# Eight more convolution taps on TensorE, and another address distance for the lower weight parts of the MLP

## The chip, the cores and the metric

The kernel runs on one core of one Trainium2 chip. The metric is device time in microseconds (us) for one launch; lower is better. The core's engines have an instruction queue each and run beside one another: TensorE (PE in the profile; its weight loads are shown apart as PEld), VectorE (DVE), ScalarE (ACT), GpSimd (POOL) and SyncE (SP), which here only issues the loads of the weights.

## The reference

A trunk of two layers over 256 tokens of width 2048, all in float32. Layer 0 mixes the tokens with a convolution module, layer 1 with latent attention; a squared-ReLU MLP of width 8192 follows each.

```python
def conv_module(h, w_pw1, b_pw1, w_dw, b_dw, ln_g, ln_b, w_pw2, b_pw2):
    u = h @ w_pw1 + b_pw1
    a, gate = jnp.split(u, 2, axis=-1)
    u = a * jax.nn.sigmoid(gate)
    u = lax.conv_general_dilated(          # causal, one filter of 31 taps per channel
        u, w_dw[:, None, :].astype(u.dtype), window_strides=(1,),
        padding=[(CONV_WIDTH - 1, 0)],
        dimension_numbers=("NWC", "WIO", "NWC"),
        feature_group_count=D_MODEL) + b_dw
    u = jax.nn.silu(layer_norm(u, ln_g, ln_b))
    return u @ w_pw2 + b_pw2
...
def sq_relu_mlp(h, w1, w2):
    return jnp.square(jax.nn.relu(h @ w1)) @ w2
...
    for layer in range(DEPTH):
...
        x = x + conv_module(...)           # layer 0; mla(...) in layer 1
        h = rms_norm(x, norm_mlp_g[layer])
        x = x + sq_relu_mlp(h, mlp_w1[layer], mlp_w2[layer])
    return rms_norm(x, final_norm_g)
```

## The kernel before

**Products in parts.** TensorE multiplies a stationary tile (128 x 128, loaded as weights, PEld) with a moving tile. Each float32 operand is split into an upper part `hi` (a copy rounded to fp32r by ScalarE) and a lower part `lo` (the remainder, a subtraction on VectorE, in the convolution mostly on GpSimd). A product is three matmuls: hi x hi, hi x lo, lo x hi. The weights stream in as `raw` tiles, three in rotation, and the parts have six buffers each (`WB`).

**Order of the work.** The order on each queue is written out by hand (`tc.manual_schedule()`), and each engine runs its own queue in that order; semaphores hold an instruction until its operands are there. Nothing is rearranged later.

**Convolution stage** (layer 0, up to about 222 us of the profile). The 2048 channels are 16 tiles of 128, c = 0 to 15. For each tile `conv_mm` does the first pointwise product (16 k-tiles x 2 halves x 3 matmuls of 128 x 256, lines 862 to 864). `glu` gates it into `ub`, a tile of 30 zeros and 256 tokens. Then the 31 taps of the filter: each tap multiplies `ub`, shifted by w, with one value per channel and adds it to a running sum. Most taps are one VectorE instruction each (`dve_tap`, line 964). Some products are made on ScalarE (`product`) and summed on GpSimd (`side_sum`); `n_side` says how many. VectorE works at up to two tiles by turns and carries a number of taps over into the next tile's turn: `rest(c)`, for the last three tiles `LAST_REST`.

The last tile, c = 15, is treated otherwise: its first 22 taps (`LAST_PE`) are matmuls on TensorE, in which the stationary tile is a diagonal matrix with the tap's 128 values (`diag`, ScalarE, line 902) and the moving tile is the shifted `ub`. These 22 products (line 912, each recorded as two matmuls) add up in the PSUM bank `last_sum`; eleven stand right after `start_sum(15)`, eleven after the transposes of tile 13. VectorE does the other taps, and line 961 adds the two sums. The transposes to token order (`to_tokens`, line 1002) and the statistics of the layer norm (`ln_stats`, line 1012, into `stats`) follow for each tile; `cn` is the tile in which ScalarE gathers the transposed result (line 1014). `keep_warm` (line 237) is a run of transposes without use.

**MLP** (both layers). `up_unit` makes one 128-wide block of the first product: eight matmuls with the upper weight part (line 519, moving tile 128 x 512, both parts of the activations side by side), sixteen with the lower part (line 517, 128 x 256) and eight more of line 519. There are 64 such units in each layer. `down_units` does the second product (lines 198 to 200, moving tile 128 x 512). While a matmul runs, the weight load of the next one runs beside it.

**Addresses.** `hi_lo` makes the lower part's tile 64 elements (256 bytes) longer than needed (`LO_GAP`), so that the part can start at any place `at` in it. In the built program these places lie at, modulo 256 bytes: `hi` and the start of the `lo` tiles 64; the activations `xt` 0 in the convolution and 64 in the MLP. "Distance" here is the address of the moving tile less that of the stationary tile, modulo 256. It is 192 in the convolution's products (0 - 64), 0 for line 519 and in the second product of the MLP (64 - 64), and 192 for line 517, where `at` is 16 elements: 64 - (64 + 64).

Of the kernel before, what the change touches and what calls it, by code (L numbers as in the profile page):

```python
# [45 lines left out]
WB = 6  # L46
LOOK = WB // 2 - 1
LAST_PE = 22
SIDE = 2
LAST_SIDE = (3, 6, 4)  # L50
JOIN = 14
LEAD = 7
REST = (16, 18, 22)
LAST_REST = (20, 17, 0)
FILL_AT = (5, 15)
ORDERS = "STSTSTOSTSTSTSTT", "TSTSTSTOSTSTSTST"
N_S, N_G = 9, 2
# [28 lines left out]
def trunk_kernel(  # L86
# [336 lines left out]
    def hi_lo(n, at=0):  # L423
        hi = wpool.tile([P, n, NB], F32R, tag="hi", name=nm("hi"), bufs=WB)
        lo = wpool.tile([P, n * NB + LO_GAP], F32R, tag="lo", name=nm("lo"), bufs=WB)
        return [hi, lo[:, at : at + n * NB].rearrange("p (a b) -> p a b", b=NB)]
# [56 lines left out]
    def mlp(layer, ssq, next_gain, finish=None, before=None, last_w1=None):  # L483
# [11 lines left out]
        def up_units(hs, q, p, extra):  # L495
# [5 lines left out]
            def up_unit(b):  # L501
                ps = []

                def chunk(h):
                    def prep(raw, parts):
                        parts[h] = [a.rearrange("p a (j n) -> p (a j) n", n=P) for a in hi_lo(2, LO_GAP // 4)]
                        split_into(parts[h], raw[:, 8 * h : 8 * h + 8, :])

                    def run(parts):
                        if not ps:  # L510
                            ps.append(acc_tile())
                        wh, wl = parts.pop(h)
                        for low in (h, 1 - h):
                            for j in range(8):
                                k = 8 * h + j
                                if low:
                                    nc.tensor.matmul(ps[0][:, :S], wl[:, j, :], xh(k), start=False, stop=False)  # L517
                                else:
                                    nc.tensor.matmul(ps[0], wh[:, j, :], xhl(k), start=k == 0, stop=k == KC - 1)  # L519

                    def out():
                        if b == 0:
                            held["u"] = u_tile()
                        nc.scalar.activation(held["u"][:, b, :], ps[0], AF.Copy)  # L524

                    if h == 0:
                        return Chunk(prep, run)
                    return Chunk(prep, run, [add, lambda: None, square, forms, part] + extra if b == 1 else [], now=out)

                unit = Unit(rows(w1, 0, KC, ((q * NPAIR + p) * 2 + b) * P, P), KC, [chunk(h) for h in range(2)])  # L530
                unit.last_read = 1
                return unit
# [270 lines left out]
    with ExitStack() as cx:  # L803
# [94 lines left out]
            return pr  # L898

        def diag(c, w):  # L900
            dg = cv2.tile([P, P], F32, tag="dg", name=nm("dg"), bufs=LAST_PE)
            nc.scalar.activation(dg, ident, AF.Copy, scale=tap(c, w))
            return dg

        dgs, last_sum, turns = [], [], {}

        def last_products(w0, w1):  # L910
            for w in range(w0, w1):
                nc.tensor.matmul(  # L912
                    last_sum[0], dgs[w], ubs[KC - 1][:, w : w + S], start=w == 0, stop=w == LAST_PE - 1
                )

        def start_sum(c):
            w = 0
            if c < KC - 1:
                pcs[c] = sum_tile()[:, :S]
                nc.scalar.activation(  # L920
                    pcs[c], ubs[c][:, 0:S], AF.Identity, bias=b_dw[:, c : c + 1], scale=tap(c, 0)
                )
                w = 1
            else:
                pcs[c] = acc_tile()[:, :S]
                o = sum_tile()[:, :S]
                last_sum.append(o)
                last_products(0, LAST_PE // 2)
                w = LAST_PE
            n = n_side(c)  # L930
            sides[c] = [product(c, w + i) for i in range(n)]
            left[c] = list(range(w + n, W))
            left[c].insert(min(JOIN, len(left[c]) - 1), None)

        def side_sum(c):
# [7 lines left out]
        def dve_tap(c):  # L943
# [9 lines left out]
                )  # L953
                return
            if not left[c]:
                if c == KC - 1:
                    half = cv2.tile([P, S], F32, tag="half", name=nm("half"), bufs=1)
                    nc.vector.scalar_tensor_tensor(
                        out=half, in0=ubs[c][:, w : w + S], scalar=tap(c, w), in1=out, op0=ALU.mult, op1=ALU.add
                    )  # L960
                    nc.vector.tensor_tensor(ca_part(c), last_sum[0], half, op=ALU.add)
                    return
                out = ca_part(c)
            nc.vector.scalar_tensor_tensor(  # L964
# [64 lines left out]
        with tc.manual_schedule():  # L1029
# [57 lines left out]
            for c in range(1, KC + 1):  # L1087
                n = UC * c
                conv_load(n + 3)
                glu(c - 1)  # L1090
                fill = ln_stats(c - 4 if c < KC else KC - 3) if c > 3 else []
                fill, copies = fill[:T], fill[T:]
# [21 lines left out]
                if c < KC:  # L1114
                    conv_mm(c, 8)
                    if c > KC - 4:
                        dgs.extend(diag(KC - 1, w) for w in range(len(dgs), min(len(dgs) + 8, LAST_PE)))
                    if c > 2:
                        to_tokens(c - 3)
                    conv_mm(c, 12)  # L1120
# [673 lines left out]
```

## Time and profile before

| | us |
|---|---|
| median of 3 runs (lowest, highest) | 1934.97 (1933.55, 1935.04) |
| the profiled execution: its own time | 1933.95 |
| the profiled execution: span of the program | 1932.1 |
| TensorE busy in the span | 1903.0 (98%) |
| VectorE busy | 1650.8 (85%) |
| ScalarE busy | 1204.7 (62%) |
| GpSimd busy | 223.3 (12%) |

The profile is of one execution. "Busy" is the time in which an engine has an instruction under way; matmuls overlap, so a busy TensorE may still be issuing slower than it could, and the distance from one matmul's start to the next one's tells more than its duration. A row of the timeline gives start, duration, engine, line, operation, tiles (out<-in) and in brackets the idle time before and what ended it. "xN" merges N instructions that follow each other.

### The profile page before, as it was taken

The page shows a single profiled execution, that of the slowest core. Times are in us where ns is not written, and L with a number is a line of the kernel's source. Part 1 is how long each engine was busy: PE and PEld are TensorE (multiplying, and loading weights), DVE is VectorE, ACT ScalarE, POOL GpSimd, SP SyncE. Part 2 cuts the span into 40 slices and gives each one's busy share as a digit, 9 for nine tenths or more (in the row PEclk, how much of TensorE's full clock was granted, in tenths as well). Part 3 has the DMA queues.
Part 4 walks back from the last instruction along what each step waited for, and adds up shares of the span by engine and source line. Part 5 has one row for each costly group of instructions (what it writes and reads, how often), then busy time and mean ns, then how long its engine had stood idle before and what let it go on. Part 6 is the DMA issues. An engine that isn't in the chain of part 4 may idle for free.

```text
span 1932.1 us, 28479 instructions
## 1 busy us (share of the span) xinstructions
PE 1903.0 (98%) x10778; PEld 1669.4 (86%) x10778; DVE 1650.8 (85%) x2374; ACT 1204.7 (62%) x1709; POOL 223.3 (12%) x183
## 2 busy tenths in 40 slices
PE   7999899999999999999999999999999999999998
PEld 7999788888888888888899998888888888888886
DVE  5999865789999999999977665657999999999887
ACT  5556654766666666666566665566666666666554
POOL 5999300000000000000001410000000000000000
PEclk9999999999999999999999999999999999999999
DMA  8676355857666667666646445765666666766663
GB/s 235 187 195 179 129 189 160 227 170 213 197 203 206 201 198 215 198 199 214 199 144 182 121 153 175 203 188 173 199 195 209 207 196 196 217 199 196 213 220 109
DMA packets 407113, 367.62 MB, mean 190 GB/s; under 512 B 15416, under 2 KB 351936, under 8 KB 406720
## 3 DMA queue, kind: packets, MB, share of 16 engines
q1 hardware_dynamic: 405952, 363.63, 62.9%
q10 hardware_dynamic: 1024, 2.17, 0.3%
q8 instruction: 84, 1.38, 0.3%
q14 instruction: 53, 0.43, 0.1%
HBM read 363.68 MB, written 2.10 MB: 189 GB/s over the span
## 4 chain that ended last, share of the span: by engine, by line
PE 88%; DVE 9%; ACT 1%; POOL 1%; issue 0%; DMA 0%; SPq 0%; DVEq 0%; ACTq 0%; POOLq 0%
PE acc L519 24%; PE acc L198 15%; PE acc L199 15%; PE acc L200 15%; PE acc L517 13%; DVE sum L964 7%; PE acc L254 1%; PE sum L912 1%; DMA xs<-in_x 0%; ACT hi L172 0%; PE acc L863 0%; PE acc L862 0%; PE acc L864 0%; PE acc L1562 0%; PE acc L1426 0%
## 5 line engine op out<-in xcount | busy, mean ns | idle before, releaser
L430 DVE TENSOR_TENSOR lo<-raw,hi 128x1024 fp32r<-128x1024 f32 (+1 forms) x512 | 570.9, 1122 | 88.5 <-ACT hi L429 88.1
L429 ACT ACTIVATE hi<-raw 128x1024 fp32r<-128x1024 f32 (+1 forms) x512 | 479.6, 970 | 66.5 <-PE acc L199 66.2
L519 PE MATMUL acc<-xt,hi 128*128 128x512 f32 x2048 | 503.2, 391 | 0.0
L519 PEld LDWEIGHTS acc<-xt,hi 128*128 128x128 f32 x2048 | 376.0, 188 | 72.7 <-ACT hi L429 0.3
L198 PE MATMUL acc<-hi,sh 128*128 128x512 f32 x930 | 362.7, 390 | 0.0
L200 PE MATMUL acc<-lo,sh 128*128 128x512 f32 x930 | 361.9, 389 | 0.0
L199 PE MATMUL acc<-hi,sl 128*128 128x512 f32 x802 | 312.0, 389 | 0.0
L517 PEld LDWEIGHTS acc<-xt,lo 128*128 128x128 f32 x2048 | 259.3, 189 | 9.8
L517 PE MATMUL acc<-xt,lo 128*128 128x256 f32 x2048 | 262.4, 281 | 0.0
L172 ACT ACTIVATE hi<-raw 128x1024 fp32r<-128x1024 f32 (+2 forms) x184 | 179.9, 1006 | 46.7 <-PE acc L199 43.0
L200 PEld LDWEIGHTS acc<-lo,sh 128*128 128x128 f32 x930 | 174.6, 188 | 36.3
L198 PEld LDWEIGHTS acc<-hi,sh 128*128 128x128 f32 x930 | 174.6, 188 | 35.9
L173 DVE TENSOR_TENSOR lo<-raw,hi 128x1024 fp32r<-128x1024 f32 (+2 forms) x118 | 132.7, 1145 | 68.4 <-ACT hi L172 62.5
L429 ACT ACTIVATE hi<-V 128x1024 fp32r<-128x1024 f32 x94 | 99.6, 1059 | 130.4 <-DVE V L725 123.2
L199 PEld LDWEIGHTS acc<-hi,sl 128*128 128x128 f32 x802 | 150.6, 188 | 31.1
L964 DVE SCALAR_TENSOR_TENSOR sum<-ub,w_dw,sum 128x256 f32<-128x256 f32 x400 | 162.8, 480 | 6.5 <-ACT sum L920 5.4
L173 POOL TENSOR_TENSOR lo<-raw,hi 128x1024 fp32r<-128x1024 f32 x66 | 157.6, 2406 | 23.5 <-ACT hi L172 22.9
L429 ACT ACTIVATE hi<-T 128x1024 fp32r<-128x1024 f32 x94 | 99.3, 1056 | 91.7 <-DVE T L713 66.8
L524 ACT ACTIVATE U<-acc 128x512 f32<-128x512 f32 x128 | 75.7, 592 | 111.9 <-PE acc L519 111.8
L862 PE MATMUL acc<-xt,hi 128*128 128x256 f32 x512 | 143.6, 280 | 0.0
L863 PE MATMUL acc<-xt,hi 128*128 128x256 f32 x512 | 142.2, 278 | 1.0 <-DVE xt L211 1.0
L864 PE MATMUL acc<-xt,lo 128*128 128x256 f32 x512 | 142.2, 278 | 0.6 <-POOL lo L173 0.6
(270 smaller groups left out, 2797.1 us busy)
## 6 DMA issues: line engine op xcount, KB each, us to landing
raw<-in_mlp_w SPq DMA_DIRECT2D x256, 1024.0 KB, 6.2
raw<-in_conv_w_pw SPq DMA_DIRECT2D x64, 512.0 KB, 5.5
raw<-in_conv_w_pw SPq DMA_DIRECT2D x16, 1024.0 KB, 5.1
raw<-in_mla_w_o SPq DMA_DIRECT2D x16, 1024.0 KB, 5.4
raw<-in_mla_w_kv_up SPq DMA_DIRECT2D x8, 1024.0 KB, 5.4
raw<-in_mla_w_in SPq DMA_DIRECT2D x8, 576.0 KB, 3.8
raw<-in_mla_w_in SPq DMA_DIRECT2D x4, 1024.0 KB, 6.9
raw<-in_mla_w_q_up SPq DMA_DIRECT2D x16, 256.0 KB, 4.9
```

The source lines that it names most:

```text
L172: nc.scalar.activation(hi, raw[:, js, :], AF.Copy)
L173: eng.tensor_tensor(lo, raw[:, js, :], hi.bitcast(F32), op=ALU.subtract)
L198: nc.tensor.matmul(ps, sh, mh, start=start, stop=False)
L199: nc.tensor.matmul(ps, sl, mh, start=False, stop=False)
L200: nc.tensor.matmul(ps, sh, ml, start=False, stop=stop)
L429: nc.scalar.activation(parts[0], src, AF.Copy)
L430: nc.vector.tensor_tensor(parts[1], src, parts[0].bitcast(F32), op=ALU.subtract)
L517: nc.tensor.matmul(ps[0][:, :S], wl[:, j, :], xh(k), start=False, stop=False)
L519: nc.tensor.matmul(ps[0], wh[:, j, :], xhl(k), start=k == 0, stop=k == KC - 1)
L862: nc.tensor.matmul(o, wh[:, bs], xh(k), start=k == 0, stop=False)
L863: nc.tensor.matmul(o, wh[:, bs], xl(k), start=False, stop=False)
L964: nc.vector.scalar_tensor_tensor(out=out, in0=ubs[c][:, w : w + S], scalar=tap(c, w), in1=pcs[c], op0=ALU.mult, op1=ALU.add)
```

## The change

**Convolution.** The last eight taps (w = 23 to 30, `BUT_ONE_PE`) of tile c = 14 leave VectorE. ScalarE makes eight more diagonal tiles, in turn c = 15, behind the last of those for tile 15. They have no buffers of their own: they lie in the last four column blocks of `cn` (two rows of blocks, eight tiles), which ScalarE fills with results only afterwards. TensorE does the eight products (`but_one_products`) behind the last pointwise product and ahead of those of tile 15, into a PSUM bank of their own. VectorE's last tap of tile 14 goes into `half`, and one addition joins it with that bank, as for tile 15 before. `LAST_REST` for turn 14 goes from 17 to 9, so that VectorE does as many steps in that turn as before (28) and eight fewer in the last turn.

**MLP.** In `up_unit`, `at` goes from 16 to 56 elements, so that the lower part starts at 32 modulo 256 and the distance of line 517 becomes 64 - 32 = 32. No instruction is added, removed or moved; VectorE's write of the lower part and TensorE's load of it have other addresses.

The lines of the file move by 1 ahead of the new code (line 887 is now 888, 517 is 518), by 5 and 6 within it (902 is now 907, 912 is 918), by 14 to 18 behind it (961 is now 975, 1012 is 1026). The rows below are from the built programs, where a name's number tells one buffer from the next.

On TensorE, at the end of the last pointwise product, before:

```order
L864 MATMUL acc_2768<-xt_102,lo_2789 128x256
L862 MATMUL acc_2769<-xt_102,hi_2788 128x256
L863 MATMUL acc_2769<-xt_102,hi_2788 128x256
L864 MATMUL acc_2769<-xt_102,lo_2789 128x256
L912 MATMUL sum_2954<-ub_2944,dg_2532 128x256
L912 MATMUL sum_2954<-ub_2944,dg_2534 128x256
L912 MATMUL sum_2954<-ub_2944,dg_2536 128x256
```

and now, with `acc_2952` as the bank for tile 14 and the diagonals in `cn`:

```order
L865 MATMUL acc_2768<-xt_102,lo_2789 128x256
L863 MATMUL acc_2769<-xt_102,hi_2788 128x256
L864 MATMUL acc_2769<-xt_102,hi_2788 128x256
L865 MATMUL acc_2769<-xt_102,lo_2789 128x256
L926 MATMUL acc_2952<-ub_2761,cn 128x256 x8
L918 MATMUL sum_2971<-ub_2961,dg_2532 128x256
L918 MATMUL sum_2971<-ub_2961,dg_2534 128x256
L918 MATMUL sum_2971<-ub_2961,dg_2536 128x256
```

The eight products stand between the last pointwise matmul and the first product of tile 15.

On VectorE, the end of the last turn before (`sum_2774` is tile 14's running sum, `acc_2953` tile 15's, `tr_2915` the transposes of tiles 12 and 13):

```order
L964 SCALAR_TENSOR_TENSOR sum_2774<-ub_2761,w_dw,sum_2774 128x256
L947 TENSOR_TENSOR acc_2953<-acc_2953,tp_2966 128x256
L964 SCALAR_TENSOR_TENSOR sum_2774<-ub_2761,w_dw,sum_2774 128x256
L1012 BN_STATS stats<-tr_2915 128x6
L964 SCALAR_TENSOR_TENSOR sum_2774<-ub_2761,w_dw,sum_2774 128x256
L1012 BN_STATS stats<-tr_2915 128x6
L964 SCALAR_TENSOR_TENSOR sum_2774<-ub_2761,w_dw,sum_2774 128x256 x5
L964 SCALAR_TENSOR_TENSOR ca_3021<-ub_2761,w_dw,sum_2774 128x256
L958 SCALAR_TENSOR_TENSOR half_3023<-ub_2944,w_dw,acc_2953 128x256
L961 TENSOR_TENSOR ca_3021<-sum_2954,half_3023 128x256
L1012 BN_STATS stats<-acc_3040 128x6 x2
```

and now (tile 15's running sum is `acc_2970`, the transposes of tiles 12 and 13 are `tr_2923`):

```order
L978 SCALAR_TENSOR_TENSOR sum_2774<-ub_2761,w_dw,sum_2774 128x256
L978 SCALAR_TENSOR_TENSOR acc_2970<-ub_2961,w_dw,acc_2970 128x256
L972 SCALAR_TENSOR_TENSOR half_3027<-ub_2761,w_dw,sum_2774 128x256
L975 TENSOR_TENSOR ca_3029<-acc_2952,half_3027 128x256
L961 TENSOR_TENSOR acc_2970<-acc_2970,tp_2983 128x256
L1026 BN_STATS stats<-tr_2923 128x6
L972 SCALAR_TENSOR_TENSOR half_3033<-ub_2961,w_dw,acc_2970 128x256
L975 TENSOR_TENSOR ca_3029<-sum_2971,half_3033 128x256
L1026 BN_STATS stats<-tr_2923 128x6
L1026 BN_STATS stats<-acc_3051 128x6 x2
```

Eight taps of tile 14 are gone, one addition (`ca_3029<-acc_2952,half_3027`) is new, and one of the two statistics of `tr_2923` now stands behind the addition that waits for `last_sum`.

On ScalarE, at the gate of tile 15 (`sg`), before:

```order
L902 ACTIVATE dg_2909<-ident,w_dw 128x128
L902 ACTIVATE dg_2911<-ident,w_dw 128x128
L902 ACTIVATE dg_2913<-ident,w_dw 128x128
L884 ACTIVATE sg_2946<-acc_2769,vecs_cv 128x256
L172 ACTIVATE hi_2949<-raw_2633 128x1024
L897 ACTIVATE tp_2966<-ub_2944,w_dw 128x256
```

and now:

```order
L907 ACTIVATE dg_2909<-ident,w_dw 128x128
L907 ACTIVATE dg_2911<-ident,w_dw 128x128
L907 ACTIVATE dg_2913<-ident,w_dw 128x128
L907 ACTIVATE cn<-ident,w_dw 128x128 x8
L885 ACTIVATE sg_2963<-acc_2769,vecs_cv 128x256
L173 ACTIVATE hi_2966<-raw_2633 128x1024
L898 ACTIVATE tp_2983<-ub_2961,w_dw 128x256
```

The eight diagonals stand ahead of the gate's sigmoid. GpSimd's and SyncE's queues are as before.

```diff
--- before.py
+++ after.py
@@ -46,12 +46,13 @@
 WB = 6
 LOOK = WB // 2 - 1
 LAST_PE = 22
+BUT_ONE_PE = 8
 SIDE = 2
 LAST_SIDE = (3, 6, 4)
 JOIN = 14
 LEAD = 7
 REST = (16, 18, 22)
-LAST_REST = (20, 17, 0)
+LAST_REST = (20, 9, 0)
 FILL_AT = (5, 15)
 ORDERS = "STSTSTOSTSTSTSTT", "TSTSTSTOSTSTSTST"
 N_S, N_G = 9, 2
@@ -503,7 +504,7 @@
 
                 def chunk(h):
                     def prep(raw, parts):
-                        parts[h] = [a.rearrange("p a (j n) -> p (a j) n", n=P) for a in hi_lo(2, LO_GAP // 4)]
+                        parts[h] = [a.rearrange("p a (j n) -> p (a j) n", n=P) for a in hi_lo(2, LO_GAP - 8)]
                         split_into(parts[h], raw[:, 8 * h : 8 * h + 8, :])
 
                     def run(parts):
@@ -898,11 +899,16 @@
             return pr
 
         def diag(c, w):
-            dg = cv2.tile([P, P], F32, tag="dg", name=nm("dg"), bufs=LAST_PE)
+            if c == KC - 2:
+                t, j = divmod(w - W + BUT_ONE_PE, 4)
+                dg = cn[:, t, (KC - 4 + j) * P : (KC - 3 + j) * P]
+            else:
+                dg = cv2.tile([P, P], F32, tag="dg", name=nm("dg"), bufs=LAST_PE)
             nc.scalar.activation(dg, ident, AF.Copy, scale=tap(c, w))
             return dg
 
         dgs, last_sum, turns = [], [], {}
+        but_one, but_one_sum = [], []
 
 
 
@@ -911,6 +917,14 @@
             for w in range(w0, w1):
                 nc.tensor.matmul(
                     last_sum[0], dgs[w], ubs[KC - 1][:, w : w + S], start=w == 0, stop=w == LAST_PE - 1
+                )
+
+        def but_one_products():
+            but_one_sum.append(acc_tile()[:, :S])
+            for i, dg in enumerate(but_one):
+                w = W - BUT_ONE_PE + i
+                nc.tensor.matmul(
+                    but_one_sum[0], dg, ubs[KC - 2][:, w : w + S], start=i == 0, stop=i == BUT_ONE_PE - 1
                 )
 
         def start_sum(c):
@@ -929,7 +943,7 @@
                 w = LAST_PE
             n = n_side(c)
             sides[c] = [product(c, w + i) for i in range(n)]
-            left[c] = list(range(w + n, W))
+            left[c] = list(range(w + n, W - BUT_ONE_PE if c == KC - 2 else W))
             left[c].insert(min(JOIN, len(left[c]) - 1), None)
 
         def side_sum(c):
@@ -953,12 +967,12 @@
                 )
                 return
             if not left[c]:
-                if c == KC - 1:
+                if c >= KC - 2:
                     half = cv2.tile([P, S], F32, tag="half", name=nm("half"), bufs=1)
                     nc.vector.scalar_tensor_tensor(
                         out=half, in0=ubs[c][:, w : w + S], scalar=tap(c, w), in1=out, op0=ALU.mult, op1=ALU.add
                     )
-                    nc.vector.tensor_tensor(ca_part(c), last_sum[0], half, op=ALU.add)
+                    nc.vector.tensor_tensor(ca_part(c), (last_sum if c == KC - 1 else but_one_sum)[0], half, op=ALU.add)
                     return
                 out = ca_part(c)
             nc.vector.scalar_tensor_tensor(
@@ -1087,6 +1101,8 @@
             for c in range(1, KC + 1):
                 n = UC * c
                 conv_load(n + 3)
+                if c == KC:
+                    but_one_products()
                 glu(c - 1)
                 fill = ln_stats(c - 4 if c < KC else KC - 3) if c > 3 else []
                 fill, copies = fill[:T], fill[T:]
@@ -1115,6 +1131,8 @@
                     conv_mm(c, 8)
                     if c > KC - 4:
                         dgs.extend(diag(KC - 1, w) for w in range(len(dgs), min(len(dgs) + 8, LAST_PE)))
+                    if c == KC - 1:
+                        but_one.extend(diag(KC - 2, w) for w in range(W - BUT_ONE_PE, W))
                     if c > 2:
                         to_tokens(c - 3)
                     conv_mm(c, 12)
```

## The prediction

> **What bounds the kernel now.** I read the chain of waits and the groups first, then the windows, then the timeline at the two places that the change touches.
>
> ```profile
> PE 88%; DVE 9%; ACT 1%; POOL 1%; issue 0%; DMA 0%; SPq 0%; DVEq 0%; ACTq 0%; POOLq 0%
> L519 PE MATMUL acc<-xt,hi 128*128 128x512 f32 x2048 | 503.2, 391 | 0.0
> L517 PE MATMUL acc<-xt,lo 128*128 128x256 f32 x2048 | 262.4, 281 | 0.0
> 410.00:740.00 330.00, 330.00 (x1699) 283.12 (x1698) 316.65 (x374) 218.40 (x266) 0.00 (x0) 1.00 0.67 202
> ```
>
> The first row is the chain by engine, the next two are groups (count, busy time, mean duration, idle time before), the last is 330 us of the first MLP: its columns are PE, PEld, DVE, ACT and POOL busy, clock, DMA share, GB/s. TensorE carries the chain and never idles before the MLP's matmuls; its clock is full. So there a matmul's pitch, from one start to the next, sets the time. VectorE has 13.35 us left in 330 (4%). The chain of waits gives the pitch:
>
> ```profile
> 481.45 1.89 PE acc L517 x16
> 483.33 3.65 PE acc L519 x16
> 486.99 1.89 PE acc L517 x16
> ...
> 496.25 0.23 PE acc L198
> ...
> 499.88 0.23 PE acc L199
> ```
>
> Sixteen of line 517 take 483.33 - 481.45 = 1.88 to 1.89 us, so 117.8 ns each; sixteen of line 519 take 486.99 - 483.33 = 3.66, so 228.6 ns each; from 496.25 to 499.88 sixteen of the second product take 3.63, so 226.9 ns.
>
> A matmul of line 517's size does not always need 117.8 ns. In the convolution the timeline has:
>
> ```profile
> 159.73 0.28 PE L864 MATMUL acc<-xt,lo 128*128 128x256 f32 x1
> ...
> 163.81 0.28 PE L864 MATMUL acc<-xt,lo 128*128 128x256 f32 x1
> ...
> 175.62 0.28 PE L862 MATMUL acc<-xt,hi 128*128 128x256 f32 x1
> ...
> 182.45 0.28 PE L863 MATMUL acc<-xt,hi 128*128 128x256 f32 x1
> ```
>
> From 159.73 to 163.81 there are 36 starts, 113.3 ns each; from 175.62 to 182.45 there are 58, 117.8 ns each. Same line group, same shape, same distance (192), full clock: this matmul has a faster and a slower rhythm, and the stretch between two sets of transposes stays in one. Line 517, also at 192, stays in the slower.
>
> The convolution's end is the other place:
>
> ```profile
> 201.37 0.28 PE L864 MATMUL acc<-xt,lo 128*128 128x256 f32 x1
> 205.94 6.70 PE L912 MATMUL sum<-ub,dg 128*128 128x256 f32 x22 [4.29 <-DVE ub L887]
> 212.47 0.38 PE L1002 MATMUL tr<-ident,ca 128*128 128x128 f32 x2
> 212.69 4.92 PE L912 MATMUL sum<-ub,dg 128*128 128x256 f32 x22
> 217.45 1.03 PE L237 MATMUL acc<-ident 128*128 128x128 f32 x8
> ```
>
> TensorE idles 4.29 us until VectorE has made tile 15's `ub`. The first eleven products then take 212.47 - 205.94 = 6.53 us, the second eleven 217.45 - 212.69 = 4.76. The windows say why (PE busy, clock, DMA share, GB/s):
>
> ```profile
> 206.00:208.00 2.00, 2.00 (x7) 0.74 0.03 8
> 208.00:210.00 2.00, 2.00 (x6) 0.50 0.00 0
> 210.00:212.00 2.00, 2.00 (x10) 0.91 0.00 0
> ```
>
> The granted clock falls to half after the gap and comes back near 211.
>
> **Convolution part: cost.** TensorE: eight products at 4.76 / 11 = 0.433 us are 3.5 us, from 201.65 (201.37 + 0.28) to about 205.1, within the gap. Their cover is VectorE, which starts `ub` only then:
>
> ```profile
> 197.17 8.31 DVE L964 SCALAR_TENSOR_TENSOR sum<-ub,w_dw,sum 128x256 f32<-128x256 f32 x21
> 205.43 0.45 DVE L887 SCALAR_TENSOR_TENSOR ub<-acc,vecs_cv,sg 128x256 f32<-128x256 f32 x1
> 217.65 0.42 DVE L961 TENSOR_TENSOR ca<-sum,half 128x256 f32<-128x256 f32 x1 [0.20 <-PE sum L912]
> ```
>
> It steps through as many taps ahead of `ub` as before, so 205.43 stays. ScalarE's part:
>
> ```profile
> 184.61 2.44 ACT L902 ACTIVATE dg<-ident,w_dw 128x128 f32<-128x128 f32 x8
> 201.74 0.47 ACT L884 ACTIVATE sg<-acc,vecs_cv 128x256 f32<-128x256 f32 x1 [2.51 <-PE acc L864]
> 214.14 0.60 ACT L1014 ACTIVATE cn<-tr 128x512 f32<-128x512 f32 x1 [4.62 <-DVE stats L1012]
> 214.74 1.28 ACT L231 ACT_TABLE_LOAD   x1
> 219.81 0.60 ACT L1014 ACTIVATE cn<-acc 128x512 f32<-128x512 f32 x1 [3.57 <-DVE stats L1012]
> 220.46 0.20 ACT L221 ACTIVATE t<-v 128x2 f32<-128x2 f32 x1
> ```
>
> Eight diagonals cost 2.44 us in an idle stretch of 2.51 ahead of `sg`, which has 3.2 us to spare before `ub`. If that cover were gone, up to 2.44 us would fall on `sg`, still within its 3.2.
>
> VectorE drops seven instructions in the last turn (eight taps less, one addition more): 7 x 0.393 = 2.8 us, with (205.43 - 197.17) / 21 = 0.393 per tap. This gains nothing: line 961 already waits 0.20 us for TensorE, and does so longer now.
>
> What gains is the clock. With TensorE idle for under 1 us instead of 4.29 I expect no fall, so the first eleven products take 4.76 instead of 6.53: 1.77 us earlier at line 961. What is late next is ScalarE. It copies `cn` of tile 13 only after both its statistics (214.14 waits for VectorE), and one of them now stands behind line 961: 217.65 - 1.77 = 215.88, two instructions of at most 0.42, copy at 216.7. Then the copy 0.60, the table load 1.28, about 0.2 for an operation of the size of the root behind it, the copy of tiles 14 and 15 at 218.8, the square root 0.65 behind it at 219.45 instead of 220.46. The layer norm waits for that root, so 1.0 us of the 1.77 is left. Ends: -1.8 if the copy needs only the first of them; +2.6 if the clock falls as before (eight products at twice 3.5 / 8 end at 208.6 and push tile 15's products from 205.94). I take -1.0, since the gap of 4.29 is the only one at whose end these rows show the fall.
>
> **MLP part: cost.** Nothing is added or moved; what changes is the rhythm of line 517, and of line 519 behind it. No row shows distance 32. The nearest rows bound it: 113.3 ns below (192, faster rhythm); above, distance 0:
>
> ```profile
> 405.51 0.28 PE L517 MATMUL acc<-xt,lo 128*128 128x256 f32 x1
> 405.63 0.40 PE L519 MATMUL acc<-xt,hi 128*128 128x512 f32 x1
> ```
>
> Here line 517 runs beside the load of an upper part (64 - 64 = 0) and takes 120 ns. So: 2048 x (113.3 - 117.8) = -9.2 us, to 2048 x (120 - 117.8) = +4.5 us. Line 519 has 228.6 - 226.9 = 1.7 ns more than the second product's matmuls of the same size and distance: 2048 x 1.7 = 3.5 us that it pays for following line 517, which may go or double. I take -9.2 and 0 for line 519: line 517 does not stand at the floor that its shape reaches elsewhere, its rhythm is the same in every chunk that the chain shows, so an address that breaks it breaks it everywhere; and two rhythms are all that the long stretches show, of which it has the slower. That is a choice between two, not a proof. A faster TensorE needs its weights sooner: in the 330 us, 512 of line 517 at 4.5 ns are 2.3 us, against VectorE's 13.35 of slack, so that is covered; without it each us would be paid back.
>
> The Trainium skill, "TensorE: Matmul & The Clock Gate", section "Step-by-step: what each phase is for", speaks against this part: TensorE has two independent read ports, and loading the next weights does not take read bandwidth from the running matmul, so the addresses' distance should not matter and the sum would be the convolution's alone. The two rhythms at one distance are no proof against it.
>
> Sum: 1933.95 - 1.0 - 9.2 = 1923.75 for an execution like the profiled one. That one lies 1.0 below the median of 1934.97, so 1924.8.
>
> **Rivals.**
> - *The distance changes nothing.* Line 517 keeps 117.8 ns; only the -1.0 stays: 1934.0. For it: conv at 192 shows both rhythms, so something else than the distance chooses. Against it: in the MLP the entry into line 517 is always the same, so there an address may well decide.
> - *Slower: lower parts at 32 meet the moving tile worse.* Line 517 at the 120 ns of distance 0 gives +4.5 - 1.0, 1938.5; with line 519's 3.5 us doubled, 1942.0. It decides from 118.3 ns on (2048 x 0.5 ns eat the 1.0), and goes past 0.2% at about 120.2. For it: 32 lies nearer to 0 than 192 (64 below 0) does. Against: 120 ns is a single matmul at a change of lines.
> - *The convolution part turns over* (clock falls all the same, +2.6): 1928.4 with the MLP's gain, 1937.6 without. A gap under 1 us speaks against it.
>
> **How the numbers follow.** 0.2% (3.9 us) is about what a measurement of this kernel tells from no change. I give the faster rhythm 0.45, no effect of the distance 0.30, a slower rhythm 0.25; the convolution's turn-over has 0.1 within each. Faster by over 0.2% (below 1931.1): 0.44. Slower by over 0.2% (above 1938.8): most of the slower rhythm, 0.21. Within: 0.35. The range: below, 1934.97 - 1.8 - 9.2 - 3.5 = 1920.5; above, into the slower case, 1941. The likeliest case's own range is 1920.5 to 1928.5.
>
> **What would show it.** In the changed kernel's profile: line 926 with eight products (sixteen records) from about 201.7 to 205.1; a granted clock of 1.00 from 206 to 212; both groups of line 918 at 4.8 us; line 975 of tile 15 near 215.9, still waiting for TensorE; the square root (line 222) near 219.4 behind ScalarE's own queue; sixteen of line 518 in 1.81 us instead of 1.89, their mean duration below 281 ns, line 520's pitch as before; VectorE's busy share in the MLP up a little, no new idle time on TensorE there. It is wrong if sixteen of line 518 take 1.88 or more, or if line 520's first matmuls after them stretch.

## The result, and the profile after

| | before | after |
|---|---|---|
| median (lowest to highest), 20 runs each, us | 1934.58 (1933.55 to 1935.71) | 1931.14 (1930.90 to 1931.75) |
| the profiled execution: time / span, us | 1933.95 / 1932.1 | 1930.93 / 1929.2 |

The ratio is 0.9983, with a 95% interval of 0.9976 to 0.9989: 3.4 us or 0.17% less. That is just inside the 0.2% that the prediction counted as no change, though the interval lies clear of 1. It had forecast 1924.8 us, 10.2 less than its median.

First the MLP. The chain of waits of the kernel after by engine, its two groups of the first product (count | busy us, mean ns | idle before), and the window 410 to 740 us (PE, PEld, DVE, ACT, POOL busy, clock, DMA share, GB/s):

```profile
PE 88%; DVE 9%; ACT 1%; POOL 1%; DMA 0%; issue 0%; SPq 0%; DVEq 0%; ACTq 0%; POOLq 0%
L520 PE MATMUL acc<-xt,hi 128*128 128x512 f32 x2048 | 504.0, 391 | 0.0
L518 PE MATMUL acc<-xt,lo 128*128 128x256 f32 x2048 | 259.7, 279 | 0.0
410.00:740.00 330.00, 330.00 (x1701) 282.69 (x1700) 317.11 (x375) 218.78 (x266) 0.00 (x0) 1.00 0.68 204
```

TensorE still carries the chain without idle time there. Of line 518 the mean duration went from 281 to 279 ns, and of line 520 it stayed. The chain of waits in the MLP (start, duration, engine, tile, line, number of instructions):

```profile
479.76 1.87 PE acc L518 x16
481.63 3.66 PE acc L520 x16
485.29 1.87 PE acc L518 x16
487.15 3.66 PE acc L520 x16
```

Sixteen of line 518 take 1.87 us; sixteen of line 517 took 1.88 to 1.89. From the trace's starts in ns, the sixteen take 1865.0 (before 1886.7), and in each unit they go, from the fifth on, through the same cycle of four pitches: 120, 113.3, 115.8 and 117.5 ns. So the faster rhythm of 113.3 ns came for one matmul in four, not for all. The last of the upper part's matmuls ahead of them has a longer pitch, 235 ns for 225.7. A whole unit (eight, sixteen and eight matmuls) takes 5527 ns instead of 5540. There are 128 units: 128 x 13 ns = 1.7 us.

Then the convolution's end. TensorE's timeline after:

```profile
201.31 3.61 PE L926 MATMUL acc<-ub,cn 128*128 128x256 f32 x16
205.78 5.02 PE L918 MATMUL sum<-ub,dg 128*128 128x256 f32 x22 [0.86 <-DVE ub L888]
210.63 0.38 PE L1016 MATMUL tr<-ident,ca 128*128 128x128 f32 x2
210.85 4.92 PE L918 MATMUL sum<-ub,dg 128*128 128x256 f32 x22
215.61 1.03 PE L238 MATMUL acc<-ident 128*128 128x128 f32 x8
```

The gap of 4.29 us has become 0.86, and the first eleven products take 210.63 - 205.78 = 4.85 us instead of 6.53. The windows (PE busy, PEld, DVE, ACT, POOL, clock, DMA share, GB/s) show the clock:

```profile
206.00:208.00 2.00, 2.00 (x10) 1.76 (x10) 2.00 (x7) 2.00 (x5) 1.18 (x2) 1.00 0.00 0
208.00:210.00 2.00, 2.00 (x11) 1.73 (x11) 2.00 (x7) 1.37 (x2) 1.92 (x3) 1.00 0.00 0
210.00:212.00 2.00, 2.00 (x12) 1.74 (x11) 1.90 (x7) 0.00 (x0) 2.00 (x2) 1.00 0.00 0
```

It stays at 1.00. VectorE's and ScalarE's timelines after:

```profile
205.21 0.51 DVE L888 SCALAR_TENSOR_TENSOR ub<-acc,vecs_cv,sg 128x256 f32<-128x256 f32 x1
215.81 0.42 DVE L975 TENSOR_TENSOR ca<-sum,half 128x256 f32<-128x256 f32 x1 [3.42 <-PE sum L918]
216.15 0.42 DVE L1026 BATCH_NORM_STATS2 stats<-tr 128x6 f32<-128x256 f32 x1
```

```profile
216.69 0.60 ACT L1028 ACTIVATE cn<-tr 128x512 f32<-128x512 f32 x1 [7.32 <-DVE stats L1026]
217.29 1.28 ACT L232 ACT_TABLE_LOAD   x1
218.69 0.58 ACT L1028 ACTIVATE cn<-acc 128x512 f32<-128x512 f32 x1
219.17 0.19 ACT L222 ACTIVATE t<-v 128x2 f32<-128x2 f32 x1
```

VectorE waits 3.42 us for TensorE's sum where it waited 0.20, and the square root comes at 219.17 instead of 220.46, behind the copy of `cn` that waits for the second statistic. The first matmul of the second pointwise product, before and after:

```profile
225.19 0.48 PE L198 MATMUL acc<-hi,sh 128*128 128x512 f32 x1
```

```profile
223.89 0.48 PE L199 MATMUL acc<-hi,sh 128*128 128x512 f32 x1
```

So 1.3 us of the gain is made by 224 us and 1.7 in the MLPs: 3.0, the difference of the two profiled executions (1933.95 - 1930.93). The remaining 0.4 of the medians' difference is that the profiled execution of before lies 0.6 below its median, that of after 0.2.

### The profile page after: what moved, and what is told of

Same layout as the page of the kernel before. It is cut to its first block, busy times and chain, and to the rows that moved or that the text cites. A ratio compares the mean times of both kernels' runs of the same rounds, so it can differ in the third digit from the quotient of the medians.

```text
span 1929.2 us, 28511 instructions
## 1 busy us (share of the span) xinstructions
PE 1904.2 (99%) x10794; PEld 1669.2 (87%) x10794; DVE 1647.4 (85%) x2367; ACT 1208.2 (63%) x1717; POOL 223.4 (12%) x183
## 4 chain that ended last, share of the span: by engine, by line
PE 88%; DVE 9%; ACT 1%; POOL 1%; DMA 0%; issue 0%; SPq 0%; DVEq 0%; ACTq 0%; POOLq 0%
PE acc L520 24%; PE acc L199 15%; PE acc L200 15%; PE acc L201 15%; PE acc L518 12%; DVE sum L978 7%; PE acc L255 1%; PE sum L918 1%; ACT hi L173 0%; DMA xs<-in_x 0%; PE acc L863 0%; PE acc L864 0%; PE acc L865 0%; PE acc L1580 0%; PE acc L1444 0%
```

## The experiments

Line numbers below are those of each run's own kernel. A time is a median with its lowest and highest, and a ratio is against the kernel before, run on the same chip.

### The two parts apart

`conv_only` is the kernel after with the old distance:

```diff
-parts[h] = [a.rearrange("p a (j n) -> p (a j) n", n=P) for a in hi_lo(2, LO_GAP - 8)]
+parts[h] = [a.rearrange("p a (j n) -> p (a j) n", n=P) for a in hi_lo(2, LO_GAP // 4)]
```

> The convolution part alone, lower parts at distance 192 as before. If the two parts are independent, the pitch of the MLP's 128x256 matmuls is that of before (sixteen in 1.89 us) and the gain is the convolution's: the profiles of before and after put the first matmul of the second pointwise product 1.3 us earlier, so 0.06% faster, about 1933.4. Rival, that the whole gain of 3.4 us is the convolution's and the MLP's profile differs by chance: 1931.1.

Measured: 1932.69 us (1932.37 to 1933.36), against 1934.47 of before; ratio 0.9990 (0.9982 to 0.9999). Its square root comes at 219.15, its first matmul of the second pointwise product at 223.86, and sixteen of line 518 take 1886 ns.

`mlp_only` is the kernel before with the new distance (the same line, the other way round).

> The MLP part alone, convolution as before. If the parts are independent: sixteen of line 517 in 1.865 us, the eighth or sixteenth of line 519 ahead of them 9 ns longer, so 128 x (21.7 - 9.2) ns = 1.6 us faster, 0.08%, about 1933.0. By the prediction's step (all of line 517 at 113.3 ns) it would be 9.2 us faster; that is out by the profile of after. Rival, a distance that changes nothing: 1934.6.

Measured: 1932.60 us (1931.92 to 1933.40); ratio 0.9991 (0.9982 to 1.0000). Sixteen of line 517 take 1865.0 ns.

So each part is worth 1.8 to 1.9 us by medians, and the sum of 3.7 agrees with the 3.4 of the whole: no dependence of the parts on each other shows. The distance does act, with nothing else changed, but by a fifth of the 9.2 us forecast. VectorE's writes of the lower parts have other addresses too, but they are not the cause: in the trace of the kernel after, the sixteen take 1864 or 1865 ns in all 128 places, both where VectorE writes no lower part beside them and where it does so all the while.

### What of the convolution part gains: the taps or the clock

`gap_filled` is the kernel before, all taps where they were, with 32 transposes of the identity tile in TensorE's gap:

```diff
                 conv_load(n + 3)
+                if c == KC:
+                    keep_warm(ident, 32)
                 glu(c - 1)
```

> Before, with 32 transposes without use (3.5 us) put into TensorE's gap ahead of tile 15's products; all taps stay on VectorE. Clock alone is the cause of the convolution's gain (the prediction's reading): no fall of the clock, both groups of eleven products at 4.8 us, line 961 about 1.7 us earlier, 1.0 us or more off the time. Rival, both are needed: the clock stays up, but line 961 then waits for VectorE, whose last tap was ready only 0.2 us ahead of TensorE, so 0.2 us off and no more. Beside it: if the spread of the times of before (1933.6 to 1935.7) comes from where the clock's fall lies, it shrinks to about that of after (1930.9 to 1931.8).

`taps_dropped` is the other half: VectorE leaves out the eight taps, and nobody does them.

```diff
-left[c] = list(range(w + n, W))
+left[c] = list(range(w + n, W - BUT_ONE_PE if c == KC - 2 else W))
...
-LAST_REST = (20, 17, 0)
+LAST_REST = (20, 9, 0)
```

> The last eight taps of tile 14 left out altogether (no diagonals, no products, VectorE as in the changed kernel but for the addition), distance 192: VectorE's saving without filling the gap. If TensorE's queue is what line 961 waits for, the clock falls, the two groups take 6.5 and 4.8 us as before, and nothing is gained; the square root comes later than before by about 0.8 us, since ScalarE's copy stands behind line 961: 0 to 0.8 us slower. Rival, VectorE's saving is the gain: 1 us or more faster.

Measured: `gap_filled` 1932.07 us (1931.80 to 1932.99), ratio 0.9989 (0.9980 to 0.9998); `taps_dropped` 1934.45 us (1934.17 to 1935.66), ratio 1.0001 (0.9992 to 1.0010). TensorE, VectorE and ScalarE with the gap filled, and the windows between (the clock is the third number from the end):

```profile
201.35 3.65 PE L237 MATMUL acc<-ident 128*128 128x128 f32 x32
205.80 5.02 PE L912 MATMUL sum<-ub,dg 128*128 128x256 f32 x22 [0.80 <-DVE ub L887]
```

```profile
206.00:208.00 2.00, 2.00 (x10) 1.76 (x10) 2.00 (x6) 2.00 (x5) 1.17 (x2) 1.00 0.00 0
208.00:210.00 2.00, 2.00 (x11) 1.75 (x10) 2.00 (x7) 1.38 (x2) 1.92 (x3) 1.00 0.00 0
```

```profile
211.48 0.41 DVE L1012 BATCH_NORM_STATS2 stats<-tr 128x6 f32<-128x256 f32 x1
...
216.11 0.42 DVE L961 TENSOR_TENSOR ca<-sum,half 128x256 f32<-128x256 f32 x1
...
218.64 0.20 ACT L221 ACTIVATE t<-v 128x2 f32<-128x2 f32 x1
```

and TensorE and VectorE with the taps left out:

```profile
205.77 7.28 PE L918 MATMUL sum<-ub,dg 128*128 128x256 f32 x22 [4.23 <-DVE ub L888]
212.88 0.38 PE L1016 MATMUL tr<-ident,ca 128*128 128x128 f32 x2
...
218.05 0.42 DVE L975 TENSOR_TENSOR ca<-sum,half 128x256 f32<-128x256 f32 x1 [3.94 <-PE sum L918]
...
226.11 0.48 PE L199 MATMUL acc<-hi,sh 128*128 128x512 f32 x1
```

The clock is the whole gain, and VectorE's saving alone is none: without the eight taps VectorE waits 3.94 us instead. With the gap filled and every tap still on VectorE, the time is 0.6 us below that of `conv_only`, and VectorE's last addition, at 216.11, waits for nothing. VectorE and TensorE are level there: VectorE's queue also moves up, since its statistics no longer wait for TensorE's transposes. Before, the first of them waited 1.20 us:

```profile
212.89 0.43 DVE L1012 BATCH_NORM_STATS2 stats<-tr 128x6 f32<-128x256 f32 x1 [1.20 <-PE tr L1002]
```

I had given it as a rival that both parts are needed and the filled gap alone brings 0.2 us; it falls.

The gap without the products also shows when the clock falls. Windows of 1 us, first of before, then with the taps left out (the third number from the end is the clock):

```profile
206.00:207.00 1.00, 1.00 (x5) 0.90 (x6) 1.00 (x4) 1.00 (x3) 0.10 (x1) 0.97 0.07 16
...
210.00:211.00 1.00, 1.00 (x6) 0.82 (x5) 1.00 (x4) 0.00 (x0) 1.00 (x1) 0.82 0.00 0
```

```profile
203.00:204.00 1.00, 0.00 (x0) 0.00 (x0) 1.00 (x3) 0.06 (x1) 0.86 (x1) 0.78 0.04 12
...
210.00:211.00 1.00, 1.00 (x5) 0.83 (x5) 1.00 (x4) 0.00 (x0) 1.00 (x1) 0.81 0.00 0
```

The windows between these stand at 0.50. A mean of 0.97 between 1 and 0.5 puts the fall at 206.94, and 0.78 at 203.56; both come back at about 210.4. So after nearly the same gap the clock stood at half for 3.4 us in one execution and for 6.8, twice that, in another, and the eleven products took 6.53 and 212.88 - 205.77 = 7.11 us. `mlp_only`, which has the same gap (4.27 us), shows the longer fall too, from 203.4 to 210.2. The Trainium skill, "TensorE: Matmul & The Clock Gate", Part 1, "What's actually happening", says that the clock is set by windows of about 3.4 us that run free of the kernel; these traces agree: 3.4 us is one such window, 6.8 are two.

The length of the fall would also explain why the runs of before spread over 2.2 us and those of after over 0.85, and the runs on record fit that. Of the 33 executions of before beside these four kernels, 18 have a mean granted clock of 0.997 (to three places) and a median of 1934.70 us, 15 have 0.998 and 1933.75. `mlp_only` and `taps_dropped`, which keep the gap, spread over 1.5 us; the kernels of five or more executions without it spread over 0.2 to 1.2. No execution without a trace shows its fall itself, so this is a fit and no proof.

It matters for `taps_dropped`, because its median depends on how many long falls it drew. Taken by clock, it is slower than before: 1934.32 us against 1933.75 at 0.998 (six executions), 1935.02 against 1934.70 at 0.997 (four). The traces agree. `mlp_only` has every tap and the same long fall, and its second pointwise product starts 0.66 us ahead of that of `taps_dropped` (226.11), with the first of tile 15's products only 0.1 us ahead:

```profile
225.45 0.48 PE L198 MATMUL acc<-hi,sh 128*128 128x512 f32 x1
```

So VectorE's saving by itself costs about half a microsecond, as expected, since ScalarE's copy of `cn` then stands behind line 975.

### Which distances are fast

Four kernels with the new convolution part, of one execution each, give each quarter of the weights and each layer a distance of its own (16 units each). `scan32`, the multiples of 32:

```diff
-parts[h] = [a.rearrange("p a (j n) -> p (a j) n", n=P) for a in hi_lo(2, LO_GAP - 8)]
+parts[h] = [a.rearrange("p a (j n) -> p (a j) n", n=P) for a in hi_lo(2, 8 * ((4 * layer + q) % 8))]
```

`scan_fine`, the multiples of 16 between them:

```diff
+FINE = (4, 12, 20, 28, 36, 44, 52, 60)
...
-parts[h] = [a.rearrange("p a (j n) -> p (a j) n", n=P) for a in hi_lo(2, LO_GAP - 8)]
+parts[h] = [a.rearrange("p a (j n) -> p (a j) n", n=P) for a in hi_lo(2, FINE[4 * layer + q])]
```

`xt_up32` is `scan32` with the activations moved up by 32 bytes, and `xt_up64` by 64 (`PAD_RIGHT` 24 and `PAD_XT` 32):

```diff
-PAD_RIGHT = 40
+PAD_RIGHT = 32
...
-PAD_XT = 16
+PAD_XT = 24
```

> The changed kernel, with another place of the lower part in each quarter of the MLP: eight distances, in the order of time 0, 224, 192, 160 (first layer), 128, 96, 64, 32 (second), 16 units each; upper parts at distance 0 throughout. Theory that the distance decides: 192 and 32 give back 1.887 and 1.865 us for the sixteen matmuls, the others differ from one another, and if 113.3 ns is to be had, one shows 1.81. Rival, that only the lower part's place within 64 bytes counts: the four multiples of 64 all take 1.887, the four others all 1.865. Rival, that neighbours in time decide and not the address: no order at all.

> The same with the eight places in between: distances 240, 208, 176, 144 (first layer), 112, 80, 48, 16 (second). If the pitch is a smooth function of the distance, each lies between its neighbours of the other scan; if 32 bytes are the grain, each equals one neighbour. If the place within 64 bytes decides, distances that differ by 64 agree (240, 176, 112, 48 and 208, 144, 80, 16).

> The activations of the MLP 32 bytes further up, so that the upper parts are at distance 32 instead of 0, and the lower parts at 32, 0, 224, 192 (first layer), 160, 128, 96, 64 (second), with the lower part at 64, 96, 128, 160, 192, 224, 0, 32 modulo 256. If the distance decides for the lower parts: 192 gives 1.887 and 32 gives 1.865 us though the places are others than in the scan before. If the place of the lower part decides: 64 modulo 256 (distance 32 here) behaves as 64 modulo 256 did there (distance 0). For the 128x512 matmuls the same question: 226.7 ns in their even stretch if distance 32 is no worse than 0, and the first five after the lower parts (232.5, 235.8, 228.4, 232.5, 230.8) tell whether their cost hangs on the upper parts' distance.

> The same with 64 bytes: upper parts at distance 64, lower parts at 64, 32, 0, 224 (first layer), 192, 160, 128, 96 (second). If the distance decides, each distance repeats its pitch of the other scans; what differs by the upper parts' distance is the entry (the last 128x512 matmul ahead, 225.7 or 235.0 ns, and the first five behind).

`scan_four` is `scan_fine` around the two best, in steps of 4 bytes:

```diff
+FINE = (51, 53, 54, 55, 50, 49, 58, 57)
```

> Distances 52, 44, 40 and 36 bytes for the lower parts in the four quarters of the first layer's weights, and 56, 60, 24 and 28 in the second layer, in place of 32 everywhere; the convolution is the changed kernel's. At multiples of 16 the sixteen lower-part matmuls took 1865.0 ns at 32, 1866.8 at 48 and 1884.2 at 64, and eight, sixteen and eight together 5527, 5507 and 5563 ns. Theory: what matters is the distance in steps of 16 bytes or more, so that 36 to 44 read as 32 (1865) and 52 to 60 as 48 (1867), and 24 and 28 as 16 (1873). Rival: every 4 bytes count, and one of these distances has the 113.3-ns rhythm throughout (1813 ns). The time says little, since the quarters differ: between 1929 and 1933 us by the theory.

Times: 1935.11, 1933.84, 1945.04 and 1941.54 us in that order, with 1935.57 of before beside them; `scan_four` 1935.51, with a median of 1934.33 of before. They mean little, as each mixes eight distances. The table has, from the starts in the traces, the time of sixteen lower-part matmuls and that of a unit, in ns, with the upper part at distance 0:

| distance | 16 | unit | distance | 16 | unit | distance | 16 | unit |
|---|---|---|---|---|---|---|---|---|
| 0 | 1912 | 5567 | 128 | 1924 | 5567 | 24 | 1897 | 5540 |
| 16 | 1873 | 5527 | 144 | 1916 | 5573 | 28 | 1905 | 5569 |
| 32 | 1865 | 5527 | 160 | 1878 | 5533 | 36 | 1933 | 5593 |
| 48 | 1867 | 5507 | 176 | 1895 | 5584 | 40 | 1900 | 5569 |
| 64 | 1884 | 5563 | 192 | 1887 | 5540 | 44 | 1876 | 5520 |
| 80 | 1886 | 5527 | 208 | 1893 | 5554 | 52 | 1964 | 5627 |
| 96 | 1920 | 5580 | 224 | 1892 | 5569 | 56 | 1908 | 5567 |
| 112 | 1904 | 5560 | 240 | 1893 | 5566 | 60 | 1897 | 5527 |

The sixteen go from 1865 to 1964 ns, 116.6 to 122.8 each, and neither of the two rhythms of the prediction stands out. Four bytes are enough to tell: 48 is the best unit, 52 the worst. The theory of `scan_four` was wrong, since 36 does not read as 32. Of its rival one half came out, that every 4 bytes count, and the other did not: none of its distances has 113.3 ns throughout.

With the activations moved 32 bytes up, the same distances come about at other places of the lower part: 32 takes 1866, 64 takes 1883, 160 takes 1878, as in the table (1865, 1884, 1878). So in most cases the distance decides and not the place. But it does not decide alone. At 192 the sixteen take 1829 ns there (113.3 each from the fourth to the fifteenth) and 1887 with the upper part at 0, and 128 takes 1898 for 1924.

The clearest case is in `xt_up64`, where upper and lower parts both stand at distance 64 in the first quarter of the first layer. There the sixteen take 1883 to 1885 and 1812 to 1814 ns by turns from one unit to the next (the first unit, at 1886, stands outside the turns). The slower ones follow an upper matmul with a pitch of 225 or 226 ns, the faster ones one of 231 or 232. These are the two rhythms of the prediction, 117.8 and 113.3 ns, at one and the same distance. So the rhythm of 113.3 ns can be had in the MLP, but it hangs on what comes ahead as well as on the distance.

The convolution, at distance 192 throughout, points the same way: between 62 and 198 us two stretches between transposes with 113.3 ns and one with 117.8 follow each other in a fixed order, in all fourteen traces. What sets that order was not looked into.

In `xt_up32` the upper part pays, since it then has a distance of 32 itself. The group and the chain of `xt_up32`:

```profile
L520 PE MATMUL acc<-xt,hi 128*128 128x512 f32 x2048 | 513.0, 395 | 0.0
```

```profile
479.96 1.87 PE acc L520 x8
481.83 1.91 PE acc L518 x16
483.74 3.73 PE acc L520 x16
487.47 1.91 PE acc L518 x16
```

Sixteen of line 520 take 3.73 instead of 3.66 us, and the kernel took 9.9 us more than `scan32`, which has the same eight distances of the lower part (9.5 more than before), in one execution each. The Trainium skill, "TensorE: Matmul & The Clock Gate", "Step-by-step: what each phase is for", which the prediction set against this part, says that TensorE has two independent read ports and that a weight load takes no read bandwidth from the running matmul. What the prediction concluded from it, that the distance should not matter, is not borne out: where only the place of the lower part differs, the sixteen move by up to 99 ns. Whether the weight load takes anything from the running matmul is not shown, and which part of the chip makes the pitch was not found.

### What the statistic behind the addition costs

`stats_ahead` moves both statistics of tile 13 ahead of line 975:

```diff
-FILL_AT = (5, 15)
+FILL_AT = (5, 13)
```

> The changed kernel with one number of the order of VectorE's last tile changed, so that both statistics of the last LayerNorm stand ahead of the addition of TensorE's sum (line 975) instead of one behind it. Theory: in the changed kernel ScalarE's copy at 216.69 us waits for the second statistic, which waits behind line 975's 3.42 us for TensorE; ahead of it, the statistics end near 212.3, the copy stands in ScalarE's idle time, and the square root comes at 218.6 instead of 219.17, as with the filled gap and the taps on VectorE (218.64): 0.5 us less, 1930.6 us. Rival: VectorE's last sum at 215.81 sets the end whichever way the statistics go, and the time stays at 1931.1.

Measured: 1930.49 us (1930.31 to 1930.83), 0.65 below the kernel after; ratio 0.9981 (0.9972 to 0.9990). ScalarE:

```profile
212.63 0.60 ACT L1028 ACTIVATE cn<-tr 128x512 f32<-128x512 f32 x1 [3.10 <-DVE stats L1026]
...
218.80 0.20 ACT L222 ACTIVATE t<-v 128x2 f32<-128x2 f32 x1
```

The copy now lies in ScalarE's idle time, and though VectorE's last addition is no earlier (215.98, after 215.81) the root is, by 0.37 us. The theory holds. The second pointwise product starts at 223.53 instead of 223.89, so 0.36 of the 0.65 us are seen there; the two medians are from different chips, and where the rest comes from was not looked into.

### A version from the findings

`best19` has distance 48, the statistics ahead, and gives VectorE three of the last tile's taps back, since it waits there:

```diff
-LAST_PE = 22
+LAST_PE = 19
-FILL_AT = (5, 15)
+FILL_AT = (5, 13)
-parts[h] = [a.rearrange("p a (j n) -> p (a j) n", n=P) for a in hi_lo(2, LO_GAP - 8)]
+parts[h] = [a.rearrange("p a (j n) -> p (a j) n", n=P) for a in hi_lo(2, 52)]
```

> The changed kernel with three numbers altered: the lower parts at distance 48 instead of 32, both statistics ahead of line 975's wait as in the run with that edit alone (1930.49 us), and nineteen instead of twenty-two of the last tile's products on TensorE, the other three back on VectorE, which waits 3.09 us for them there (215.98 us). Theory: at 48 a unit of eight, sixteen and eight matmuls takes 5507 ns instead of 5527, and there are 128 units: 2.6 us; three products in two halves of 11 records each less are 3 of 22 of 10.0 us, 1.37 us of TensorE ahead of the last sum, while VectorE's three taps take 1.2 us of its wait, so that the sum comes near 214.6: 1.3 us. Together 1930.5 - 2.6 - 1.3 = 1926.6 us. Rival: the units at 48 were seen in one layer's quarter each and follow a different entry in the other, so that only half of the 2.6 us comes (1927.9); or the statistics and transposes behind line 975 set the end, so that the 1.3 us fall to 0.5 (1927.4).

`filled48` is the kernel before with the filled gap and distance 48, no tap moved (the expectation calls the transposes those of zeros; they are of the identity tile, as in `gap_filled`).

> The kernel before with no tap moved: thirty-two transposes of zeros fill TensorE's gap, as in the run with the filled gap (1932.07 us), and the lower parts stand at distance 48. Theory: unit 5507 instead of 5540 ns, 128 times: 4.2 us less, 1927.8 us; the eight taps on TensorE are worth nothing in themselves, and what remains against the kernel with nineteen products (1926.6) is the order of the statistics and the three products. Rival: distance 48 has its short unit only with the convolution's changed part ahead of it, since the entry differs: 1929 to 1930 us.

Measured: `best19` 1926.34 us (1926.18 to 1926.98), ratio 0.9961 (0.9947 to 0.9974); `filled48` 1927.73 us (1927.65 to 1927.84), ratio 0.9967 (0.9955 to 0.9980). The expected 1926.6 and 1927.8 came out. VectorE, ScalarE and TensorE at the end of the convolution of `best19`:

```profile
214.29 0.42 DVE L975 TENSOR_TENSOR ca<-sum,half 128x256 f32<-128x256 f32 x1
...
217.11 0.20 ACT L222 ACTIVATE t<-v 128x2 f32<-128x2 f32 x1
...
221.84 0.48 PE L199 MATMUL acc<-hi,sh 128*128 128x512 f32 x1
```

and its chain in the MLP:

```profile
482.77 1.87 PE acc L518 x16
484.64 3.64 PE acc L520 x16
```

The addition no longer waits; the second pointwise product starts 2.05 us earlier than in the kernel after. The units take 5507 ns, 20 less, mostly in line 520 behind the lower parts (3.64 for 3.66): 2.6 us. Together 4.6 of the 4.8 us between the medians. Only here does moving the taps beat the filled gap without the move, by 1.4 us against `filled48`. How much of that is the eight taps and how much the three given back was not taken apart.

## Why the prediction was right or wrong

**MLP, wrong in size: the term of -9.2 us measured -1.7.** The step that failed is "two rhythms are all that the long stretches show", with "so an address that breaks it breaks it everywhere". The second half held: all 128 units changed alike. The first did not: the convolution's stretches had shown two rhythms of a larger set, and distance 32 gave a third, a cycle of four; its sixteen take 116.6 ns each. The prediction called it a choice between two; in the scans the sixteen take anything from 113 to 123 ns each. What could have been read beforehand is that neither end of the price range was measured at this distance, so that a value within it, such as -1.7, was as good a forecast as the lower end. That the MLP got faster at all was luck: of the 23 other distances in the table 7 have a shorter unit than 192, and nothing in the prediction told 32 from the rest.

**Line 519, taken as 0.** Behind the lower parts that held: the first matmul there has a pitch of 232.5 ns for 233.3, and the others keep theirs. What the sum left out is the matmul ahead of them, 235 ns instead of 225.7. It takes 9 of the 22 ns that the sixteen gain: 128 x 9 ns = 1.2 us. That is a third of the bound named ("3.5 us that may go or double"), but in another place.

**Convolution, right in its steps.** The eight products lie in the gap, the diagonals do not hold up the gate (`sg` at 201.57, before 201.74), the clock stays at 1.00, line 975 stands at 215.81 (forecast 215.88), the copy of `cn` at 216.69 (216.7), the root at 219.17 (219.45, since the root follows the last copy by 0.48 us and not 0.65). The gain is 1.3 us in the profiled execution against 1.0 forecast, and 1.8 by the medians of `conv_only`. The profiled execution of before had the shorter of the two falls of the clock; `conv_only` lies 1.1 us below the executions of before with a mean clock of 0.998, like that one, and 2.0 below those with 0.997.

**"This gains nothing" of VectorE's seven instructions**: right (`taps_dropped` 1934.45 against 1934.47, and 0.3 to 0.6 slower where executions of the same mean clock are compared). That ScalarE's copy behind the second statistic is late next was also right; it costs 0.37 us up to the root and 0.65 by medians (`stats_ahead`).

**The rivals.** That the distance changes nothing came near in time (1934.0 forecast for it, 1931.14 measured; the turn-over with the MLP's gain, 1928.4, is as near) and is wrong as a mechanism: `mlp_only` reads 1865.0 for 1886.7. The slower rhythm exists, at 0 (1912) and at others, but not at 32: that 32 lies nearer to 0 said nothing about it. The turn-over of the convolution did not come.

## What to carry to other kernels

When a profile shows two values of a pitch, they are two points and no list of all that there are; an untried address gets a price inside the bounds, and a scan in one launch (another address for each quarter of the weights) settles it for less than an argument. Price a move by what it takes off the path: here the idle gap's effect on the clock was the whole gain of the convolution's part, cheap transposes got it without the move, and the engine that was relieved only waited longer. After such a move, see what stands in the queue behind the new wait, and give back work to the engine that now waits.

## What the runs showed of the hardware

- The pitch of the fp32r matmuls of 128 x 256 depends on the address of the moving tile less that of the stationary one, in steps as small as 4 bytes: 1867 ns for sixteen at 48, 1964 at 52. With the upper part at distance 0, the cycle of pitches is the same from unit to unit at each distance, and the matmuls of the upper part next to it take part (a unit of 5507 to 5627 ns).
- The distance is not all: at 64 in `xt_up64` sixteen take 1884 and 1813 ns by turns, behind a matmul with a pitch of 226 and of 232 ns.
- Matmuls of 128 x 512 took 226 to 227 ns at distance 0 (`before`, from the sixth behind the lower parts on) and mostly 231 to 236 at 32 (`xt_up32`).
- Transposes keep the clock up: with 32 of them in the gap the granted clock was 1.00 from 204 to 212 us, where it fell to 0.50 without them. The Trainium skill, "TensorE: Matmul & The Clock Gate", "Part 4: PE-mode transpose", says that transposes do not count as work of TensorE for the clock in the same way; this run shows that here they were enough.
- The half clock lasted 3.4 us in one execution and 6.8 in two others, behind gaps of 4.29, 4.23 and 4.27 us.
